# A trunk inference step: the adaLN products in 2 MB units with a weight buffer of their own

## The chip, the core and the metric

The kernel runs on one core of a Trainium2 chip. The metric is the time of one execution on the device, in microseconds: the median of three runs is 1693.69 us (1690.03 to 1694.74). One more execution was taken with the hardware profiler; all times of instructions here come from it.

## What is computed

Two groups of tokens, 128 context tokens and 256 latent tokens, go through two layers of width 1024. Each layer is a half-step SwiGLU feed-forward block, a mixer (differential attention, latent attention and a state-space path with one common input and one common output product) and a second feed-forward block. What enters each part is normed and then modulated, and what leaves it is gated, by nine vectors a layer that come from a conditioning vector:

```
def adaln(cvec, l, p):
    m = jax.nn.silu(cvec) @ p['w_ada'][l] + p['b_ada'][l]
    return m.reshape(cvec.shape[0], N_MOD, D_MODEL)

def trunk_layer(x, mod, l, p, pos, ctx):
    sh1, sc1, g1, sh2, sc2, g2, sh3, sc3, g3 = [mod[:, i, None, :] for i in range(N_MOD)]
    nw = p['norm_w'][l]
    x = x + 0.5 * g1 * swiglu(modulate(rms_norm(x, nw[0]), sh1, sc1), p['ffn_w_in'][l, 0], p['ffn_w_out'][l, 0])
    m, new_ctx = mixer(modulate(rms_norm(x, nw[1]), sh2, sc2), l, p, pos, ctx)
    x = x + g2 * m
    x = x + 0.5 * g3 * swiglu(modulate(rms_norm(x, nw[2]), sh3, sc3), p['ffn_w_in'][l, 1], p['ffn_w_out'][l, 1])
    return x, new_ctx
```

The weight `w_ada` is 1024 x 9216 in float32 for each of two layers, 72 MB in all. There are only two conditioning vectors, one for each token group, so the products have two useful columns against 75 MB of weights to be read. The shift, scale and gate of a part must exist before that part needs them, and not earlier.

## The kernel before

Activations lie transposed: 128 features on the partitions, 384 tokens along the rows, eight blocks. The large weights come as float32 and each is split into two float32r halves, `whi` by ScalarE and `wlo` by VectorE or GpSimd (`split`, L234 and L213), with two buffers for each half (`SPB`). Each product is three matmuls (`mm3`, L239 to L241). All weight loads go through `load` (L246), on the queue of SyncE (SP), into one ring of three 1 MB buffers, `raw`.

The adaLN products are made piece by piece as fillers between other work. `ada_steps` makes a list of units; each unit loads 1 MB of `w_ada` into a buffer of the ring `raw` and then multiplies. The conditioning vectors are the stationary operand, padded to 32 columns, and the weights stream. Four column groups of 32 of the array hold four stretches of columns at the same time (`ps[32*q:32*q+32]`, `q` = 0 to 3), one matmul each in turn. With 2048 output columns to a group a matmul has 512 columns and a unit four matmuls; with 1024 it has 256 and a unit eight. After the last unit of a group ScalarE copies the accumulator `adaps` (`ad`), TensorE transposes it in pieces (`adapt`) and VectorE adds the bias into `adaT`.

The very first 2048 columns are made in the opening (`start`, tile `araw`). Then 12 units are fillers of the first feed-forward block of layer 0 (eight of them together with steps that prepare tables for the state-space path), 32 of the first mixer, two of each of the next two feed-forward blocks, and 16 of the second mixer. `fill` takes the next filler off the list: the feed-forward blocks call it after each up or down step, the mixers after some input products and in each step of the attention loop.

That is the order in which the program is written. Which instruction an engine really gets next is set when the program is built: a scheduler lists the instructions of each engine and may move an independent instruction past others. Each engine works through its list in order. `tc.issue_after(x)` forbids the scheduler to place an instruction before `x`. A tile with `bufs=1` has a single buffer: who writes it next must wait until all readers of the last content are done.

The state-space path needs a table `Wi` that is written to memory and read back in another layout (`kext`, from L739; two DMAs on GpSimd's queue, tiles `kd` and `Wi`). Its first reader is the product `py` in the mixer (L1065).

Of the kernel before, what the change touches and what calls it, by code (L numbers as in the profile page):

```python
# [20 lines left out]
DEPTH = 2  # L21
# [44 lines left out]
def _layout(inp):  # L66
# [5 lines left out]
    wa = w[:, :, :8192].reshape(2, 8, 128, 4, 2048).transpose(0, 3, 1, 2, 4).reshape(2, 32, 128, 2048)  # L72
    wb = w[:, :, 8192:].reshape(2, 4, 2, 128, 1024).transpose(0, 1, 3, 2, 4).reshape(2, 4, 128, 2048)
    d['wada'] = np.concatenate([wa, wb], 1)
    for z in range(2):
        wc = w[:, :, 4096 + 1024 * z:5120 + 1024 * z].reshape(2, 4, 2, 128, 1024).transpose(0, 1, 3, 2, 4)
        d['wada'][:, 16 + 4 * z:20 + 4 * z] = wc.reshape(2, 4, 128, 2048)
    d['wada'][0, :8] = w[0, :, :2048].reshape(8, 128, 2, 8, 128).transpose(3, 1, 0, 2, 4).reshape(8, 128, 2048)
# [98 lines left out]
def trunk(ctx, tc, I, O):  # L177
# [8 lines left out]
    def bank(name):  # L186
        return psp.tile([128, 512], F32, tag="P", name=name)
# [5 lines left out]
    def SMV(n):  # L193
        return sm[:, SM[n][0]:SM[n][1]]
# [23 lines left out]
    def add(out, a, b, eng=None):  # L218
        return tt(out, a, b, ALU.add, eng)
# [13 lines left out]
    def act(out, a, f, **k):  # L233
        S.activation(out, a, f, **k)  # L234
# [8 lines left out]
    def load(src, n=2048):  # L243
        raw = wp.tile([128, 2048], F32, tag="raw", name="raw", bufs=RAWB)
        with tc.issue_after(cur.pop('dma')) if 'dma' in cur else nullcontext():
            nc.sync.dma_start(raw[:, :n], src)  # L246
        return raw

    def split(view, k, n, eng=None):
# [25 lines left out]
    adaT = [cst.tile([128, 72, 2], F32, name=f"adaT{l}") for l in range(DEPTH)]  # L275
    bada = SMV('b_ada').rearrange("p (l b) -> p l b", l=2)

    def ada_steps(l, g):
        w = 512 if g in (0, 1, 3) else 256
        units = w // 64  # L280
        row = int(8 * g)
        st = {}

        def unit(u):
            raw = load(I['wada'][l, row + u])
# [3 lines left out]
            for kk in range(8 // units):  # L289
                k = u * (8 // units) + kk  # L290
                for q in range(4):
                    c0 = kk * 1024 + q * w
                    T.matmul(ps[32 * q:32 * q + 32, 0:w], conds[:, k, :], raw[:, c0:c0 + w],  # L293
                             start=(k == 0), stop=(k == 7))
            if u == units - 1:
                ad = sp.tile([128, 512], F32, tag="ad", name="ad")
                act(ad[:, :w], ps[:, :w], AF.Copy)
                pt = bank("adapt")
                nch = w // 128
                for c in range(nch):  # L300
                    T.transpose(pt[:, c * 128:(c + 1) * 128], ad[:, c * 128:(c + 1) * 128], ident)
                b0 = 2 * row
                pv = pt[:, 0:nch * 128].rearrange("p (c q x) -> p q c x", c=nch, q=4)[:, :, :, 0:2]
                ov = adaT[l][:, b0:b0 + 4 * nch, :].rearrange("p (q c) x -> p q c x", c=nch)
                bv = bada[:, l, b0:b0 + 4 * nch].rearrange("p (q c) -> p q c", c=nch)
                for q in range(4):
                    add(ov[:, q], pv[:, q], bv[:, q, :, None].broadcast_to([128, nch, 2]))

        return [lambda u=u: unit(u) for u in range(units)]

    def mods(l, i):
        s = cst.tile([128, 8, 2], F32, name=f"mod{l}{i}")
# [333 lines left out]
    def s5_prep(l, s5p):  # L646
# [85 lines left out]
        def kext():  # L732
            o, bd = P['O'], work['bd']
            pk = bank("kext")
            pv = pk.rearrange("p (h d j) -> p h d j", h=2, d=2)
            for gp in range(8):
                for d in range(2):
                    for r in range(2):
                        T.matmul(pv[32 * (gp % 4):32 * (gp % 4) + 32, gp // 4, d, :],  # L739
                                 bd[:, r, d * 8 + gp].rearrange("p a c -> p (a c)"),  # L740
                                 o[:, r, d * 8 + gp, d:d + 8, :].rearrange("p j c -> p (j c)"),
                                 start=(r == 0), stop=(r == 1))
            kx = cur['fp'].tile([128, 2, 15, 16], F32, tag="s5raw", name="kx")
# [12 lines left out]
            nc.gpsimd.dma_start(wi.rearrange("p h g n -> p (h g) n"), win)  # L756
# [37 lines left out]
        steps += [lambda d=d, hf=hf: gtab(d, hf) for d in range(2) for hf in range(4)]  # L794
        steps += [etab]
        return P, steps

# [602 lines left out]
    def start(stp):  # L1400
# [4 lines left out]
        bv = bada[:, 0, 0:16].rearrange("p (z k) -> p z k", z=2)  # L1405
        pss = [[bank("up"), bank("up")] for _ in range(NF)]
        nx = 0
        for k in range(NB):
            while nx < min(NB, k + 1 + k // 2):
                nc.sync.dma_start(xT[:, nx], xv[:, nx])  # L1410
                norm.block(nx)
                nx += 1
            raw = stp.tile([128, 2048], F32, tag="araw", name="araw", bufs=4)
            nc.sync.dma_start(raw, I['wada'][0, k])
# [43 lines left out]
    def both(f, g):  # L1458
        return lambda: (f(), g())

    SKIP = 0
    g1 = ada_steps(0, 1)
    fillers += g1[:SKIP] + [both(f, g) for f, g in zip(g1[SKIP:], prep)] + inter(ada_steps(0, 2), prep[8 - SKIP:])

    N1, N2 = 16, 18
    
    for l in range(DEPTH):
        nx = {}

        def after_last(k):  # L1470
            if k == 0:
                nx['n'] = Norm()
            nx['n'].tail(k)
            act(xT[:, k], xT[:, k], AF.Copy, scale=SMV('fnw')[:, k:k + 1])

        def after_h(l2, i2):
            def f(k):
                if k == 0:
                    nx['n'] = Norm()
                    nx['s'], nx['sh'] = mods(l2, i2)  # L1480
                    nx['h'] = new_h()
                nx['n'].block(k)
                ffn_h_block(nx['h'], nx['s'], nx['sh'], k)
            return f

        last = l + 1 == DEPTH
        if l:
            open_ffn()
            fillers += a1[N2:]
# [7 lines left out]
        mixer(l, nx['h'], nx['n'], P, s5stack, after_h(l, 2), lazily(lambda: gates(l, 1)))  # L1497
        if not last:
            s5stack, P, prep = open_s5(l + 1)
            mid = a1[N1:N2]  # L1500
            fillers += [both(f, g) for f, g in zip(mid, prep)] + mid[len(prep):] + prep[len(mid):]
# [11 lines left out]
        (nc.sync if i % 2 else nc.scalar).dma_start(yv[:, a:b], xT[:, a:b])  # L1513


_NAMES = ('xT', 'wada', 'wfi', 'wfo', 'win', 'wout', 'wsm', 's5', 'small', 'lam', 'kc', 'vc', 'ckvc', 'kpec', 'const')


# [12 lines left out]
```

## Time and profile before

| what | us |
|---|---|
| median of three runs | 1693.69 |
| profiled execution | 1691.62 |
| its span, first to last instruction | 1689.1 |
| opening | 0 to 49.3 |
| layer 0, first feed-forward block | 49.3 to 338.7 |
| layer 0, mixer | 338.7 to 588.7 |
| layer 0, second feed-forward block | 588.7 to 882.6 |
| layer 1, first feed-forward block | 882.6 to 1165.6 |
| layer 1, mixer | 1165.6 to 1392.5 |
| layer 1, second feed-forward block, final norm | 1392.5 to 1689.1 |

The blocks are told apart by the first `up`, `pj` or `up` matmul of each. The profile shows each float32 matmul of the adaLN as two records, and a float32r matmul or a transpose as one. PE is TensorE's matmul side and PEld its weight loads, DVE is VectorE, ACT ScalarE, POOL GpSimd, SP SyncE. The ends of matmuls are modelled and overlap the next start, so that a run's time is read from the merged row.

### The profile page before, as it was taken

Reading aid. Unit: us, or ns where it says so; the run is one execution under the profiler, and the core shown is the slowest. Engines: PE = TensorE matmul, PEld = TensorE weight load, DVE = VectorE, ACT = ScalarE, POOL = GpSimd, SP = SyncE. Lnnn points to the kernel's source line nnn. Section 1 sums busy time; section 2 is a strip of 40 time slices with the busy share of each in tenths; the row PEclk is TensorE's granted clock in tenths of the full one; section 3 lists DMA queues with packets and bytes.
Section 4 is the critical chain, followed back from the end, with each engine's and each line's share of the span. In section 5 each row is a group of like instructions: output and inputs, shape, how many; then the busy total and the mean of one; then the engine's idle time right before and its main releaser. Section 6 shows DMA issues by size and latency. Waiting matters only on the chain.

```text
span 1689.1 us, 26142 instructions
## 1 busy us (share of the span) xinstructions
PE 1638.3 (97%) x10144; PEld 1491.4 (88%) x10144; DVE 1099.7 (65%) x2752; ACT 690.1 (41%) x1295; POOL 157.5 (9%) x220
## 2 busy tenths in 40 slices
PE   7999999999999999999999999999998899999997
PEld 6888999998545889999999999999974589999997
DVE  5974577758456788577575555557655766555555
ACT  4332333433455543333343333334345654333333
POOL 1220010023001400000000000001311140000000
PEclk9999999999999999999999999999999999999998
DMA  9564543443477443353344333435337133333432
GB/s 376 194 222 154 146 148 105 145 175 117 154 275 276 159 140 135 125 137 120 100 152 173 119 126 112 143 94 172 133 113 251 51 116 114 124 121 118 138 97 84
DMA packets 45931, 251.47 MB, mean 149 GB/s; under 512 B 5600, under 2 KB 10576, under 8 KB 23920
## 3 DMA queue, kind: packets, MB, share of 16 engines
q1 hardware_dynamic: 41360, 241.12, 41.4%
q0 software_dynamic: 2144, 4.54, 1.1%
q10 hardware_dynamic: 2304, 4.15, 0.8%
q8 instruction: 79, 1.29, 0.3%
q14 instruction: 44, 0.36, 0.1%
HBM read 246.73 MB, written 3.05 MB: 148 GB/s over the span
## 4 chain that ended last, share of the span: by engine, by line
PE 87%; DVE 6%; ACT 3%; DMA 2%; issue 2%; POOL 0%; ACTq 0%; SPq 0%; DVEq 0%; POOLq 0%
PE up L239 15%; PE up L241 14%; PE up L240 14%; PE down L239 7%; PE down L241 7%; PE down L240 7%; PE adaps L293 4%; PE pj L239 2%; PE pj L241 2%; PE pj L240 2%; DMA raw<-in_wada 1%; PE pout L241 1%; PE pout L239 1%; PE pout L240 1%; PE po L1174 1%
## 5 line engine op out<-in xcount | busy, mean ns | idle before, releaser
L234 ACT ACTIVATE whi<-raw 128x1024 fp32r<-128x1024 f32 (+3 forms) x360 | 332.5, 926 | 658.8 <-PE up L240 333.5
L239 PE MATMUL up<-hh,whi 128*128 128x386 f32 x1408 | 474.4, 342 | 7.8 <-ACT whi L234 4.0
L241 PE MATMUL up<-hh,wlo 128*128 128x386 f32 x1408 | 478.5, 340 | 0.6 <-DVE wlo L213 0.6
L240 PE MATMUL up<-hl,whi 128*128 128x386 f32 x1408 | 478.5, 340 | 0.0
L213 DVE TENSOR_TENSOR wlo<-raw,whi 128x1024 fp32r<-128x1024 f32 (+2 forms) x318 | 347.7, 1093 | 49.3 <-ACT whi L234 46.5
L239 PEld LDWEIGHTS up<-hh,whi 128*128 128x128 f32 x1408 | 266.2, 190 | 15.6 <-ACT whi L234 5.3
L241 PEld LDWEIGHTS up<-hh,wlo 128*128 128x128 f32 x1408 | 265.7, 189 | 9.0 <-DVE wlo L213 2.2
L240 PEld LDWEIGHTS up<-hl,whi 128*128 128x128 f32 x1408 | 266.3, 189 | 1.6 <-issue 1.1
L241 PE MATMUL down<-hidh,wlo 128*128 128x384 f32 x704 | 236.3, 336 | 0.0
L239 PE MATMUL down<-hidh,whi 128*128 128x384 f32 x704 | 235.8, 335 | 0.0
L240 PE MATMUL down<-hidl,whi 128*128 128x384 f32 x704 | 235.3, 334 | 0.0
L231 DVE SCALAR_TENSOR_TENSOR xTt<-down,gate,xTt 128x256 f32<-128x256 f32 (+1 forms) x256 | 95.1, 414 | 114.9 <-PE down L241 114.9
L466 DVE COPY bb<-up 128x2 f32<-128x2 f32 x176 | 27.8, 159 | 190.0 <-PE up L241 189.5
L241 PEld LDWEIGHTS down<-hidh,wlo 128*128 128x128 f32 x704 | 132.1, 188 | 1.1 <-issue 0.6
L239 PEld LDWEIGHTS down<-hidh,whi 128*128 128x128 f32 x704 | 132.2, 188 | 1.0 <-ACT whi L234 0.8
L240 PEld LDWEIGHTS down<-hidl,whi 128*128 128x128 f32 x704 | 132.2, 188 | 0.0
L213 DVE TENSOR_TENSOR t<-up,R 128x384 f32<-128x384 f32 x176 | 95.5, 549 | 3.3 <-ACT R L234 3.2
L293 PE MATMUL adaps<-raw,conds 128*32 128x256 f32 (+1 forms) x704 | 84.7, 498 | 3.6 <-DMA raw<-in_wada 3.6
L239 PE MATMUL pj<-hh,whi 128*128 128x386 f32 (+1 forms) x240 | 83.2, 348 | 0.9 <-ACT whi L234 0.7
L234 ACT ACTIVATE hidh<-sl 128x384 fp32r<-128x384 f32 x88 | 46.1, 524 | 91.1 <-DVE sl L231 91.1
L241 PE MATMUL pj<-hh,wlo 128*128 128x386 f32 (+1 forms) x240 | 82.1, 343 | 1.2 <-DVE wlo L213 1.2
L240 PE MATMUL pj<-hl,whi 128*128 128x386 f32 (+1 forms) x240 | 81.5, 341 | 0.0
(268 smaller groups left out, 1953.0 us busy)
## 6 DMA issues: line engine op xcount, KB each, us to landing
raw<-in_wfi SPq DMA_DIRECT2D x85, 1024.0 KB, 4.9
raw<-in_wada SPq DMA_DIRECT2D x64, 1024.0 KB, 5.7
raw<-in_wfo SPq DMA_DIRECT2D x32, 768.0 KB, 4.2
raw<-in_wfo SPq DMA_DIRECT2D x32, 640.0 KB, 3.9
raw<-in_win SPq DMA_DIRECT2D x14, 1024.0 KB, 4.8
araw<-in_wada SPq DMA_DIRECT2D x8, 1024.0 KB, 9.8
raw<-in_wout SPq DMA_DIRECT2D x16, 512.0 KB, 3.5
wr<-in_wfi SPq DMA_DIRECT2D x8, 384.0 KB, 9.7
```

The costliest lines, as they stand in the source:

```text
L213: return (eng or V).tensor_tensor(out, a, b, op=op)
L231: return V.scalar_tensor_tensor(out, a, s, b, op0=op0, op1=op1)
L234: S.activation(out, a, f, **k)
L239: T.matmul(out, whi, xhi, start=first, stop=False)
L240: T.matmul(out, whi, xlo, start=False, stop=False)
L241: marks.append(T.matmul(out, wlo, xhi, start=False, stop=last).ins)
L293: T.matmul(ps[32 * q:32 * q + 32, 0:w], conds[:, k, :], raw[:, c0:c0 + w], start=(k == 0), stop=(k == 7))
L466: V.tensor_copy(bb[:, z], ps[z][:, NT:NT + 2])
L1174: T.matmul(po[64 * h2:64 * h2 + 64, 0:256], vt[:, kt, 128 * b + 64 * h2:128 * b + 64 * h2 + 64], wTs[h2][:, kt, :], start=(kt == 0), stop= ...
```

## The change

The columns after the first 2048 of layer 0 are one list over both layers: 16384 columns in eight groups of 2048. A group is four units; a unit is a quarter of the contraction (two blocks of 128 rows), 2 MB, eight matmuls of 512 columns. The weights go into a tile `araw` with one buffer, not into the ring `raw`. The load of the next unit is a filler of its own behind each unit (`ada_load`), placed after the latest load of the ring. In the feed-forward blocks a unit's matmuls may not move ahead of the last `mm3`; in the mixers they are free (`cur['mixing']`).

```
-    def ada_steps(l, g):
-        w = 512 if g in (0, 1, 3) else 256
-        units = w // 64
+    def ada_load():
+        if pairs:
+            g, u = pairs.pop(0)
+            raw = wp.tile([128, 2, 4, 512], F32, tag="araw", name="araw", bufs=1)
+            with tc.issue_after(cur['load']):
+                nc.sync.dma_start(raw.rearrange("p k q n -> p (k q n)"), I['wada'][g, u])
+            ahead.append((g, u, raw))
...
+            with nullcontext() if cur.get('mixing') else tc.issue_after(marks[-1]):
+                for kk in range(2):
+                    for q in range(4):
+                        T.matmul(ps[32 * q:32 * q + 32], conds[:, 2 * u + kk, :], raw[:, kk, q],
+                                 start=(u == 0 and kk == 0), stop=(u == 3 and kk == 1))
+            if u == 3:
+                ad = sp.tile([128, 512], F32, tag="ad", name="ad")
+                act(ad, ps, AF.Copy)
+                pt = bank("adapt")
...
+        out = []
+        for u in range(4):
+            out += [lambda u=u: unit(u), ada_load]
+        return out
...
-            nc.gpsimd.dma_start(kd.rearrange("c h g n -> g c h n"), kx.rearrange("p h j c -> p h (j c)"))
+            nc.scalar.dma_start(kd.rearrange("c h g n -> g c h n"), kx.rearrange("p h j c -> p h (j c)"))
...
+        def kwin():
+            nc.scalar.dma_start(P['Wi'].rearrange("p h g n -> p (h g) n"), work['win'])
...
-    fillers += g1[:SKIP] + [both(f, g) for f, g in zip(g1[SKIP:], prep)] + inter(ada_steps(0, 2), prep[8 - SKIP:])
+    ada = [ada_steps(g) for g in range(8)]
+    w = ada[0] + ada[1]
+    fillers += w[:8] + [both(f, g) for f, g in zip(w[8:], prep)] + prep[8:]
...
-            fillers += ada_steps(0, 2.5) + ada_steps(0, 3) + ada_steps(0, 4)
-            a1 = ada_steps(1, 0) + ada_steps(1, 1) + ada_steps(1, 2)
-            fillers += a1[:N1]
+            fillers += ada[2] + ada[3] + ada[4] + ada[5]
         else:
-            fillers += ada_steps(1, 2.5) + ada_steps(1, 3) + ada_steps(1, 4)
+            fillers += ada[6] + ada[7]
+        cur['mixing'] = True
...
-    nc = bacc.Bacc("TRN2", target_bir_lowering=False, num_devices=1)
+    nc = bacc.Bacc("TRN2", target_bir_lowering=False, num_devices=1, dynamic_dma_scratch_size=1024)
```

So eight units (16 MB) stand in the first feed-forward block, 16 in the first mixer, eight in the second, none in the two blocks between. As the scheduler lists them, the ninth unit goes ahead into the first block and the 25th into the first mixer: nine, sixteen and seven. The two DMAs of `Wi` go to ScalarE's queue, the second one four preparation steps later, and the scratch that GpSimd's DMAs use shrinks to 1024 bytes.

The list of TensorE in the attention of the first mixer, before (`sc` scores, `wtp` transposes of the softmax, `po` the product with the values, `pk` keys; one adaLN unit is x4):

```order
L1212 MATMUL sc<-kT,qT 128x384 x4
L293 MATMUL adaps<-raw,conds 32x512 x4
L1167 MATMUL wtp<-co,e 128x128 x3
L1252 MATMUL sc<-kTh,qT_4454 128x384
L293 MATMUL adaps<-raw,conds 32x512 x4
L1167 MATMUL wtp<-co,e 128x128
L1237 MATMUL pk<-ckT,wsm 128x512
```

The same engine and part of the attention in the changed kernel, where one unit is x8 and x16 is two units with nothing between:

```order
L1224 MATMUL sc<-kT,qT 128x128 x4
L1189 MATMUL po<-wTp,vt_4436 64x128
L300 MATMUL adaps<-araw,conds 32x512 x8
L1179 MATMUL wtp<-co,e 128x128 x3
L300 MATMUL adaps<-araw,conds 32x512 x16
L307 MATMUL adapt<-co,ad 128x128 x4
L1264 MATMUL sc<-kTh,qT_4437 128x128
L1179 MATMUL wtp<-co,e 128x128 x3
```

Three units now stand within three transposes, where before units of half the size had scores and transposes between them.

Somewhat later on TensorE in the same attention, changed kernel (`npr` the norm's products, `pout` the output product):

```order
L1264 MATMUL sc<-kTh,qT_4437 128x384
L1179 MATMUL wtp<-co,e 128x128 x3
L1011 MATMUL npr<-co,tiny 64x128 x6
L300 MATMUL adaps<-araw,conds 32x512 x16
L307 MATMUL adapt<-co,ad 128x128 x4
L235 MATMUL pout<-hh_4655,whi 128x384
```

Here two units stand in a row again, and the transposes of the group follow them directly.

The queue of SP from the small weights of the mixer on, before (`raw` is the ring of three):

```order
L246 DMA raw<-in_wsm 128x1152
L246 DMA raw<-in_wada 128x2048 x16
L246 DMA raw<-in_wout 128x1024
L246 DMA raw<-in_wada 128x2048 x5
L246 DMA raw<-in_wout 128x1024
L246 DMA raw<-in_wada 128x2048 x4
L246 DMA raw<-in_wout 128x1024 x6
```

The same stretch of SP's queue in the changed kernel:

```order
L242 DMA raw<-in_wsm 128x1152
L242 DMA raw<-in_wout 128x1024 x2
L283 DMA araw<-in_wada 128x4096
L242 DMA raw<-in_wout 128x1024
L283 DMA araw<-in_wada 128x4096 x3
L242 DMA raw<-in_wout 128x1024
L283 DMA araw<-in_wada 128x4096 x7
L242 DMA raw<-in_wout 128x1024
L283 DMA araw<-in_wada 128x4096 x3
L242 DMA raw<-in_wout 128x1024 x3
```

The adaLN loads are half as many, and the output product's weights stand between them.

## Rows read from the trace of the kernel before

**Rows 1.** The page's head, busy us by engine, and GB/s in 40 slices.

```profile
span 1689.1 us, 26142 instructions
PE 1638.3 (97%) x10144; PEld 1491.4 (88%) x10144; DVE 1099.7 (65%) x2752; ACT 690.1 (41%) x1295; POOL 157.5 (9%) x220
...
GB/s 376 194 222 154 146 148 105 145 175 117 154 275 276 159 140 135 125 137 120 100 152 173 119 126 112 143 94 172 133 113 251 51 116 114 124 121 118 138 97 84
```

**Rows 2.** Busy time of each engine by stage; first column the length, last the clock.

```profile
core 0: us, PE busy (x) PEld busy (x) DVE busy (x) ACT busy (x) POOL busy (x), PEclk, DMA share, GB/s
...
338.70:588.70 250.00, 241.01 (x1610) 172.04 (x1609) 158.54 (x464) 112.22 (x278) 52.84 (x52) 0.98 0.54 191
...
882.60:1165.60 283.00, 283.00 (x1632) 280.61 (x1631) 168.64 (x335) 109.10 (x168) 4.13 (x17) 1.00 0.39 132
1165.60:1392.50 226.90, 212.24 (x1474) 167.12 (x1473) 149.11 (x439) 110.11 (x277) 51.40 (x51) 0.98 0.39 134
```

**Rows 3.** The same by stage for instructions on the tile adaps alone.

```profile
49.30:338.70 289.40, 18.76 (x128) 3.82 (x128) 0.00 (x0) 0.98 (x2) 1.00 0.48 158
338.70:588.70 250.00, 43.34 (x320) 8.48 (x320) 0.00 (x0) 2.56 (x5) 0.98 0.54 191
588.70:882.60 293.90, 2.14 (x32) 0.83 (x32) 0.00 (x0) 0.00 (x0) 1.00 0.41 132
882.60:1165.60 283.00, 2.75 (x32) 0.94 (x32) 0.00 (x0) 0.39 (x1) 1.00 0.39 132
1165.60:1392.50 226.90, 17.70 (x192) 4.71 (x192) 0.00 (x0) 1.39 (x3) 0.98 0.39 134
```

**Rows 4.** Timeline of PE: start, time of a run, the run (two records a matmul).

```profile
49.36 1.06 PE L293 MATMUL adaps<-raw,conds 128*32 128x512 f32 x8
...
493.61 1.92 PE L293 MATMUL adaps<-raw,conds 128*32 128x512 f32 x16
...
496.70 1.05 PE L293 MATMUL adaps<-raw,conds 128*32 128x512 f32 x4
```

**Rows 5.** DMA issues: tile, queue, count, size, median us from issue to landing.

```profile
raw<-in_wfi SPq DMA_DIRECT2D x85, 1024.0 KB, 4.9
raw<-in_wada SPq DMA_DIRECT2D x64, 1024.0 KB, 5.7
raw<-in_wfo SPq DMA_DIRECT2D x32, 768.0 KB, 4.2
...
Wi<-kd POOLq DMA_DIRECT2D x2, 1024.0 KB, 22.5
```

**Rows 6.** Timeline of PE: three transposes of the softmax in the first mixer.

```profile
537.90 0.49 PE L1167 MATMUL wtp<-co,e 128*128 128x128 f32 x3
```

**Rows 7.** Busy time by stretch within the first mixer, columns as in Rows 2.

```profile
412.00:416.00 4.00, 2.58 (x23) 1.58 (x22) 3.88 (x9) 2.85 (x8) 0.00 (x0) 0.98 0.10 25
416.00:420.00 4.00, 4.00 (x24) 3.15 (x22) 0.18 (x1) 1.87 (x4) 0.59 (x1) 0.60 0.97 328
450.00:500.00 50.00, 46.28 (x300) 22.04 (x298) 26.45 (x99) 28.80 (x80) 1.54 (x3) 0.97 0.73 264
500.00:560.00 60.00, 58.69 (x374) 32.06 (x373) 39.40 (x139) 30.93 (x93) 10.01 (x10) 1.00 0.69 247
```

**Rows 8.** Timeline of PE: an adaLN run that waits, with idle time and releaser.

```profile
515.41 0.82 PE L1167 MATMUL wtp<-co,e 128*128 128x128 f32 x6
517.27 1.07 PE L293 MATMUL adaps<-raw,conds 128*32 128x512 f32 x8 [1.05 <-DMA raw<-in_wada]
```

**Rows 9.** Timeline of PE: transposes directly behind a group's last matmul.

```profile
198.73 1.06 PE L293 MATMUL adaps<-raw,conds 128*32 128x256 f32 x14
200.29 0.44 PE L301 MATMUL adapt<-co,ad 128*128 128x128 f32 x2 [0.49 <-ACT ad L234]
```

**Rows 10.** Reader and loader of Wi: count, min/median/max ns, first and last start.

```profile
L1065 PE MATMUL py<-Wi,U x64: 272/310/449, 415.3 to 1252.0; 128*48 128x128 f32 x64
```

More of the change, by code (lines that the diff above doesn't have):

```diff
@@ L71, in _layout @@
     w = a['w_ada']
[L72 to L78, printed above, removed]
+    d['wada0'] = w[0, :, :2048].reshape(8, 128, 2, 8, 128).transpose(3, 1, 0, 2, 4).reshape(8, 128, 2048)
+    w = np.concatenate([w[0, :, 2048:], w[1]], 1)
+    d['wada'] = w.reshape(4, 2, 128, 8, 2048).transpose(3, 0, 2, 1, 4).reshape(8, 4, 128, 4096)
     d['wfi'] = a['ffn_w_in'].reshape(2, 2, 8, 128, 2, NJ, 128).transpose(0, 1, 5, 3, 2, 4, 6).reshape(2, 2, NJ, 128, 2048)
@@ L245, in load @@
         with tc.issue_after(cur.pop('dma')) if 'dma' in cur else nullcontext():
-            nc.sync.dma_start(raw[:, :n], src)
+            cur['load'] = nc.sync.dma_start(raw[:, :n], src).ins
         return raw
@@ L274, in trunk, with ada_steps @@
     act(conds[:, :, 0:2], SMV('cond').rearrange("p (k c) -> p k c", c=2), AF.Silu)
-    adaT = [cst.tile([128, 72, 2], F32, name=f"adaT{l}") for l in range(DEPTH)]
-    bada = SMV('b_ada').rearrange("p (l b) -> p l b", l=2)
-    def ada_steps(l, g):
-        w = 512 if g in (0, 1, 3) else 256
-        units = w // 64
-        row = int(8 * g)
+    adaA = cst.tile([128, 144, 2], F32, name="adaA")
+    adaT = [adaA[:, 72 * l:72 * l + 72] for l in range(DEPTH)]
+    bada = SMV('b_ada')
+    pairs = [(g, u) for g in range(8) for u in range(4)]
+    ahead = []
+    def ada_load():
[5 more added lines that the diff above has]
+            ahead.append((g, u, raw))
+    def ada_steps(g):
         st = {}
         def unit(u):
-            raw = load(I['wada'][l, row + u])
+            if not ahead:
+                ada_load()
+            g_, u_, raw = ahead.pop(0)
+            assert (g, u) == (g_, u_)
             if u == 0:
@@ L288, in unit @@
             ps = st['ps']
-            for kk in range(8 // units):
-                k = u * (8 // units) + kk
-                for q in range(4):
[L292 to L309, printed above, removed]
+            with nullcontext() if cur.get('mixing') else tc.issue_after(marks[-1]):
[7 more added lines that the diff above has]
+                pt = bank("adapt")
+                for c in range(4):
+                    T.transpose(pt[:, c * 128:(c + 1) * 128], ad[:, c * 128:(c + 1) * 128], ident)
+                b0 = 16 + 16 * g
+                pv = pt.rearrange("p (c q x) -> p q c x", c=4, q=4)[:, :, :, 0:2]
+                ov = adaA[:, b0:b0 + 16, :].rearrange("p (q c) x -> p q c x", c=4)
+                bv = bada[:, b0:b0 + 16].rearrange("p (q c) -> p q c", c=4)
+                for q in range(4):
+                    add(ov[:, q], pv[:, q], bv[:, q, :, None].broadcast_to([128, 4, 2]))
+        out = []
+        for u in range(4):
+            out += [lambda u=u: unit(u), ada_load]
+        return out
     def mods(l, i):
@@ L755, in kext @@
             win = bass.AP(tensor=src.tensor, offset=src.offset, ap=[[16, 8], list(src.ap[0]), list(src.ap[1]), [1, 128]])
-            nc.gpsimd.dma_start(wi.rearrange("p h g n -> p (h g) n"), win)
+            work['win'] = win
             P['Wi'] = wi
+        def kwin():
+            nc.scalar.dma_start(P['Wi'].rearrange("p h g n -> p (h g) n"), work['win'])
         def etab():
@@ L793, in s5_prep @@
         steps += [kext]
-        steps += [lambda d=d, hf=hf: gtab(d, hf) for d in range(2) for hf in range(4)]
+        steps += [lambda d=d, hf=hf: (gtab(d, hf), kwin() if (d, hf) == (0, 3) else None) for d in range(2) for hf in range(4)]
         steps += [etab]
@@ L1404, in start @@
         av = adaT[0][:, 0:16, :].rearrange("p (z k) x -> p z k x", z=2)
-        bv = bada[:, 0, 0:16].rearrange("p (z k) -> p z k", z=2)
+        bv = bada[:, 0:16].rearrange("p (z k) -> p z k", z=2)
         pss = [[bank("up"), bank("up")] for _ in range(NF)]
@@ L1412, in start @@
                 nx += 1
-            raw = stp.tile([128, 2048], F32, tag="araw", name="araw", bufs=4)
-            nc.sync.dma_start(raw, I['wada'][0, k])
+            raw = stp.tile([128, 2048], F32, tag="araw0", name="araw0", bufs=4)
+            nc.sync.dma_start(raw, I['wada0'][k])
             wr = stp.tile([128, NF, 256], F32, tag="wr", name="wr", bufs=4)
@@ L1459, in both @@
         return lambda: (f(), g())
-    SKIP = 0
-    g1 = ada_steps(0, 1)
-    fillers += g1[:SKIP] + [both(f, g) for f, g in zip(g1[SKIP:], prep)] + inter(ada_steps(0, 2), prep[8 - SKIP:])
-    N1, N2 = 16, 18
+    ada = [ada_steps(g) for g in range(8)]
+    w = ada[0] + ada[1]
+    fillers += w[:8] + [both(f, g) for f, g in zip(w[8:], prep)] + prep[8:]
     for l in range(DEPTH):
@@ L1488, in trunk @@
             open_ffn()
-            fillers += a1[N2:]
         ffn(l, 0, h, norm, lazily(lambda: gates(l, 0)), after_h(l, 1), 0, () if l else pss)
         if l == 0:
-            fillers += ada_steps(0, 2.5) + ada_steps(0, 3) + ada_steps(0, 4)
-            a1 = ada_steps(1, 0) + ada_steps(1, 1) + ada_steps(1, 2)
-            fillers += a1[:N1]
-        else:
-            fillers += ada_steps(1, 2.5) + ada_steps(1, 3) + ada_steps(1, 4)
+            fillers += ada[2] + ada[3] + ada[4] + ada[5]
+        else:
+            fillers += ada[6] + ada[7]
+        cur['mixing'] = True
         mixer(l, nx['h'], nx['n'], P, s5stack, after_h(l, 2), lazily(lambda: gates(l, 1)))
+        cur['mixing'] = False
         if not last:
             s5stack, P, prep = open_s5(l + 1)
-            mid = a1[N1:N2]
-            fillers += [both(f, g) for f, g in zip(mid, prep)] + mid[len(prep):] + prep[len(mid):]
+            fillers += prep
         open_ffn()
@@ L1513, in trunk @@
         (nc.sync if i % 2 else nc.scalar).dma_start(yv[:, a:b], xT[:, a:b])
-_NAMES = ('xT', 'wada', 'wfi', 'wfo', 'win', 'wout', 'wsm', 's5', 'small', 'lam', 'kc', 'vc', 'ckvc', 'kpec', 'const')
+_NAMES = ('xT', 'wada0', 'wada', 'wfi', 'wfo', 'win', 'wout', 'wsm', 's5', 'small', 'lam', 'kc', 'vc', 'ckvc', 'kpec', 'const')
 def kernel(**inputs):
```

## The prediction

> **What bounds the kernel now.** I read the totals first: TensorE is busy 97% of a span of 1689.1 us, the next engine (VectorE) 65% [rows 1]. So a change counts if it shortens or stops TensorE. Next the table by stage [rows 2]: the feed-forward block of the second layer is busy for all its 283.00 us, the first mixer for 241.01 of 250.00, the second for 212.24 of 226.90. Even in the mixers little is free: 9.0 and 14.7 us. The same stretches for the adaLN accumulator alone [rows 3] say what the work to be moved costs: 18.76, 43.34, 2.14, 2.75 and 17.70 us. The timeline tells how it costs [rows 4]: the profile shows two records for each of these matmuls, which go to four column groups in turn; a run of four matmuls of 512 columns (eight records) takes 1.06 us, of two matmuls 1.05, of eight 1.92. Short runs pay for groups that stand empty. Last the loads [rows 5]: 1 MB lands 4.9 us after its issue, 0.75 MB after 4.2; an adaLN load, often beside others, after 5.7.
>
> **Matmul runs.** Columns and bytes stay; 704 records become 512, and a unit becomes eight matmuls. Where the new order leaves a unit whole it costs 1.92 us, in pieces the sum of its runs. By that order: first feed-forward block, nine units, eight whole and one as 5+1+2: 8 x 1.92 + 1.92 + 2 x 1.05 = 19.4, against 18.76: +0.6. First mixer, sixteen units: twelve whole (23.0), then 3+3+2 (3.15), 1+7 (2.97), 1+1+1+5 (5.07), 5+1+2 (4.02): 38.2 against 43.34: -5.1. The two blocks between the mixers lose theirs: -2.1 and -2.8. Second mixer, seven units, five whole (9.6), 2.97 and 5.07: 17.6 against 17.70: -0.1. Sum -9.5; bounds -23 (all 32 units whole: 61.4 against 84.7) and -4.9 (the blocks between alone). TensorE is nearly full there, so I count it all.
>
> **The wait that is added.** The old loads share a ring of three 1 MB buffers. The new buffer is one: a unit's 2 MB load can be issued only when the last matmul of the unit before has read it, and TensorE takes instructions in order. So two units closer together than a load takes make TensorE stand. The order of the first mixer has this at three places: a unit, three transposes, a unit, a unit directly behind it; later once more two in a row. What is queued behind them is the attention itself (scores, transposes, the output product), and with it the next block. A 2 MB load is not in the trace. Bounds: 2.1 MB at the busiest rate of any slice, 376 GB/s [rows 1], takes 5.6 us without any fixed part; twice 5.7 is 11.4. From 0.75 to 1 MB the landing grows by 0.7 us [rows 5], 2.8 per MB, so I take 4.9 + 2.8 = 7.7. The three transposes hide 0.49 [rows 6]: 7.2 + 7.7 + 7.7 = 22.6 us. Could TensorE have been idle there anyway? From 500 to 560 us it is busy 58.69 of 60.00 [rows 7], so hardly 1 us. And the ring of three already ends one wait with an adaLN load, 1.05 us at 517.27 [rows 8], while DMA is busy 0.69 to 0.73 of the time [rows 7]. The Trainium skill, page "DMA: Bandwidth & Descriptors", section "Anatomy of one DMA — SWDGE (gpsimd) path", gives about 2.0 us plus bytes at 436 GB/s, as an estimate 6.8 us a load, 20 us for the three and 1710 for the kernel. For 1 MB it would give 4.4 where rows 5 have 4.9 on the hardware queue, so I leave it.
>
> The other neighbours in the attention stand further apart; between none (0) and one whole load (8) of exposure in sum, I take +3. In the feed-forward blocks two units have 96 matmuls between them, at 283.00 / 1632 = 0.173 us [rows 2] 16.6 us, more than a load: 0. If that cover went, each of eight units could cost the 7.7.
>
> **Transposes behind the last unit.** At four places the four transposes of a group now follow its last matmul directly and wait for ScalarE's copy. In the old order that happens once visibly: 0.49 us of idle time [rows 9]. Four such, with the wider copy, 2 to 4; one is paid already: +2.
>
> **The clock.** In the first mixer the granted clock is 0.98, a loss of 5 us over 250 [rows 2]. From 412 to 416 us TensorE is busy 2.58 of 4.00, and from 416 to 420 the clock is 0.60 with the engine busy throughout [rows 7]: 3.2 us at the lower of 1.2 and 2.4 GHz, 1.6 us lost. Three waits longer than that idle time should bring three such stretches, 4.8, partly inside the wait itself, and some of the old ones may move: 0 to +10, I take +3. The Trainium skill speaks against the change here: "TensorE: Matmul & The Clock Gate", section "HAM oscillation — how this bites in real kernels", tells of bursts of matmuls that each start at the low clock because a DMA wait stands before them. By that rule the term is the full 4.8 and the kernel 1715. Rows 7 agree that idle time goes before the fall; no run shown here has a wait as long.
>
> **The rest.** While TensorE stands, the other engines catch up: -1 (0 to -3, since only some 1 us of later idle time is there to win). The table DMA Wi takes 22.5 us to land [rows 5] and moves from GpSimd's queue to ScalarE's, later in the block, but its first reader starts only at 415.3 [rows 10], some 77 us into the mixer: 0. ScalarE waits for the first of the two DMAs with splits queued behind it that TensorE needs; two split buffers hide that: 0 to +5, taken 0. The smaller scratch for GpSimd's DMAs is not visible in the trace; GpSimd is busy 52.84 of 250.00 [rows 2]: 0 to +3, taken 0. The ring of three that now belongs to the other weights alone can gain nothing where TensorE is never idle: 0 to -2, taken 0.
>
> **Sum.** -9.5 + 22.6 + 3 + 2 + 3 - 1 = +20.1 us. The profiled execution took 1691.6 (its span of 1689.1 and 2.5 around it); that gives 1711.7. The median of the three runs, 1693.7, lies 2.1 higher, so the same sum on it gives 1713.8; I say 1713.
>
> **Rivals.**
> (a) The load chain sets the pace of the whole attention, not three places of it. Loads of 11.4 us (beside weight loads on the same queue, which also stand behind waiting adaLN loads): 3 x 11.4 = 34, the other neighbours 12, clock 5: -9.5 + 34 + 12 + 2 + 5 = +43, 1735. It decides once a 2 MB load takes over some 10 us. For it: DMA busy 0.69 to 0.73 in this stretch. Against: few other loads are left there, and 1 MB alone lands in 4.9.
> (b) Faster. The waits fall where the attention's own chain is late, so that the two units in a row cost nothing: -9.5, and 2 from the clock, 1680 to 1682. It decides once less than 9.5 of the 22.6 us is exposed. For it: 9.0 us idle in the first mixer, and units stand in pairs where a scheduler saw nothing else to issue. Against it: 58.69 of 60.00 busy in just that stretch.
> (c) Both cancel: the saving gets half way to its bound (-16), the loads cost their lower bound of 5.6 each (17), the small terms 2: +3, 1694 to 1697. It needs pieces that pack as well as whole units, against rows 4.
>
> **How the numbers follow.** Forecast 0.62, its own range 1703 to 1724 (waits 16 to 29 and the small terms); (a) 0.18; (b) 0.10; (c) 0.10. Some 0.3% (5 us) is what a measurement of this kernel can tell from no change. Slower by more: forecast, (a) and a little of (c), 0.82. Same: most of (c), 0.08. Faster: (b), 0.10. The range runs from 1694, inside (c), to 1734, nearly the whole of (a); left out are (b) and a tail above.
>
> **What would show it.** The waits of TensorE should list adaLN matmuls waiting for the araw load, three of them 7 to 9 us long between some 510 and 600 us, and little else new; the first mixer 265 to 280 us long, the second within 3 us of 226.90, the two blocks between them some 2 us shorter each. The adaLN records should be 512, busy some 75 us outside the opening (before 84.7). The 2 MB load should land in about 7.7. Granted clock in the first mixer 0.97 or less. I am wrong if no wait exceeds 4 us, if the first mixer is not longer than 250, or if the blocks between grow.

## The result and the profile after

The changed kernel takes 1731.3 us (median; runs from 1729.7 to 1741.3) against 1692.2 for the kernel before on the same chip: ratio 1.0243, 95% interval 1.0200 to 1.0285, slower by 39 us. The forecast was 1713 with a range of 1694 to 1734: the sign and the place are right, the size is half. The result lies inside the stated range and above the forecast's own range, 1703 to 1724.

The profiled execution of the first series took 1741.3 us, ten more than the median. I ran the kernel once more for a profile near the median (e5: 1731.5 us, span 1729.7), and make the sum with that one. Both show the same waits.

The totals of e5, which answer to [rows 1]:

```profile
span 1729.7 us, 25680 instructions
PE 1637.5 (95%) x9952; PEld 1488.2 (86%) x9952; DVE 1096.8 (63%) x2740; ACT 688.6 (40%) x1292; POOL 153.2 (9%) x216
```

TensorE is busy 0.8 us less than before in a span 40.6 us longer: the loss looks like nothing but idle time, until the clock is read below. By stage, e5, columns as in [rows 2] (first feed-forward block, first mixer, the two blocks between, second mixer, last block):

```profile
49.30:342.30 293.00, 289.03 (x1719) 268.74 (x1720) 202.51 (x486) 108.34 (x173) 33.37 (x51) 1.00 0.51 173
342.30:632.00 289.70, 244.93 (x1545) 172.71 (x1545) 156.18 (x457) 111.65 (x278) 53.43 (x52) 0.93 0.45 164
632.00:923.50 291.50, 289.17 (x1694) 286.54 (x1693) 216.51 (x528) 116.74 (x187) 4.69 (x22) 1.00 0.41 126
923.50:1204.00 280.50, 280.07 (x1598) 279.61 (x1598) 168.33 (x330) 108.71 (x167) 4.15 (x17) 1.00 0.38 125
1204.00:1432.90 228.90, 213.07 (x1392) 165.13 (x1391) 147.45 (x435) 109.78 (x275) 51.17 (x51) 0.99 0.34 123
```

First mixer 289.7 against 250.0: +39.7, and the clock fell from 0.98 to 0.93. The first block is 3.6 us longer, the blocks between 2.4 and 2.5 shorter, the second mixer 2.0 longer. The adaLN accumulator alone, for [rows 3], in the first block and the two mixers:

```profile
49.30:342.30 293.00, 19.39 (x144) 1.00 0.51 173
342.30:632.00 289.70, 47.06 (x256) 0.93 0.45 164
1204.00:1432.90 228.90, 18.99 (x112) 0.99 0.34 123
```

The first block has the 19.4 of the forecast to the tenth. The first mixer has 47.06 where 38.2 were forecast. The group of the adaLN matmuls and its load, from the page of e5 (busy, mean ns, then the idle time before them; last the median landing):

```profile
L300 PE MATMUL adaps<-araw,conds 128*32 128x512 f32 x512 | 85.4, 683 | 27.5 <-DMA araw<-in_wada 27.5
...
araw<-in_wada SPq DMA_DIRECT2D x32, 2048.0 KB, 7.5
```

And where the longest of those waits lie: the timeline of TensorE in the first profile of the changed kernel (start, length, the run; in brackets the idle time and what ended it):

```profile
527.47 1.92 PE L300 MATMUL adaps<-araw,conds 128*32 128x512 f32 x16
529.33 0.55 PE L1179 MATMUL wtp<-co,e 128*128 128x128 f32 x3
537.10 3.61 PE L300 MATMUL adaps<-araw,conds 128*32 128x512 f32 x16 [7.22 <-DMA araw<-in_wada]
548.23 3.64 PE L300 MATMUL adaps<-araw,conds 128*32 128x512 f32 x16 [7.53 <-DMA araw<-in_wada]
...
583.06 3.64 PE L300 MATMUL adaps<-araw,conds 128*32 128x512 f32 x16 [1.10 <-DMA araw<-in_wada]
594.54 3.64 PE L300 MATMUL adaps<-araw,conds 128*32 128x512 f32 x16 [7.84 <-DMA araw<-in_wada]
```

Three waits of 7.22, 7.53 and 7.84 us, 22.6 in sum: just the places and the sum that the forecast gave (22.2 in e5). Read the second column too: the unit that didn't wait takes 1.92 us, those behind a wait 3.6, the same run at half speed (1.2 of 2.4 GHz). So the loss of the clock stands in the busy time of the engine, not in its idle time, and the totals hide it.

All waits for a load in the first mixer, e5 and then the kernel before (sum, times, longest):

```profile
PE adaps L300 <- DMA araw<-in_wada: 26.5, 7, 7.7
PE adaps L293 <- DMA raw<-in_wada: 2.1, 3, 1.0
```

### The profile page after: what moved, and what is told of

The parts are those of the page before. It is cut to its first block, busy times and chain, and to the rows that moved or that the text cites. A ratio compares the mean times of both kernels' runs of the same rounds, so it can differ in the third digit from the quotient of the medians.

```text
span 1739.5 us, 25680 instructions
## 1 busy us (share of the span) xinstructions
PE 1648.2 (95%) x9952; PEld 1495.0 (86%) x9952; DVE 1096.8 (63%) x2740; ACT 688.7 (40%) x1292; POOL 151.6 (9%) x216
## 4 chain that ended last, share of the span: by engine, by line
PE 84%; DVE 7%; DMA 3%; ACT 3%; issue 2%; POOL 0%; SPq 0%; DVEq 0%; ACTq 0%; POOLq 0%
PE up L235 13%; PE up L236 13%; PE up L237 13%; PE down L235 7%; PE down L237 7%; PE down L236 7%; PE adaps L300 5%; DMA araw<-in_wada 3%; PE pj L235 2%; PE pj L237 2%; PE pj L236 2%; PE pout L237 1%; PE sc L1224 1%; PE pout L235 1%; PE pout L236 1%
## 5 line engine op out<-in xcount | busy, mean ns | idle before, releaser
L300 PE MATMUL adaps<-araw,conds 128*32 128x512 f32 x512 | 87.9, 702 | 26.9 <-DMA araw<-in_wada 26.9
```

The source lines that it names most:

```text
L300: T.matmul(ps[32 * q:32 * q + 32], conds[:, 2 * u + kk, :], raw[:, kk, q], start=(u == 0 and kk == 0), stop=(u == 3 and kk == 1))
```

## The experiments

My theory, T1: a single buffer makes TensorE stand a whole load wherever a unit follows a unit. Rivals: the loads as a whole pace the mixers (R2), the free placement (R3), the small parts of the change (R4), the adaLN matmuls lowering the clock by themselves (R1).

**e1: the same memory as two buffers of 1 MB.**

```diff
-raw = wp.tile([128, 2, 4, 512], F32, tag="araw", name="araw", bufs=1)
+raw = [wp.tile([128, 4, 512], F32, tag="araw", name="araw", bufs=2) for _ in range(2)]
...
-nc.sync.dma_start(raw.rearrange("p k q n -> p (k q n)"), I['wada'][g, u])
+for kk in range(2):
+    nc.sync.dma_start(raw[kk].rearrange("p q n -> p (q n)"), I['wada'][g, u, :, 2048 * kk:2048 * kk + 2048])
...
-T.matmul(ps[32 * q:32 * q + 32], conds[:, 2 * u + kk, :], raw[:, kk, q],
+T.matmul(ps[32 * q:32 * q + 32], conds[:, 2 * u + kk, :], raw[kk][:, q],
```

> The changed kernel, with the unit's 2 MB brought by two 1 MB loads into two buffers of 1 MB each (the same memory): the first half can be refilled when the first four of a unit's eight matmuls have run. T1 (one buffer of 2 MB makes TensorE stand a whole load time of 7.7 us wherever a unit follows a unit, and the low clock comes behind those waits): adaLN waits fall from 26.9 us to under 8, the half-speed stretches of the first mixer from some 55 us to under 20, time 1692 to 1705. R1 (adaLN matmuls themselves, in runs of eight, make the clock fall): waits go, clock stays at 0.91 to 0.95 in the first mixer, time 1705 to 1715. R2 (the total of 64 MB in the mixers is too much for the loads): waits stay at 20 us or more, time 1725 to 1735.

Measured: 1689.2 us, ratio to before 0.9989 (0.9978 to 1.0000). The group of the adaLN matmuls on the page of e1:

```profile
L301 PE MATMUL adaps<-araw,conds 128*32 128x512 f32 x512 | 79.8, 611 | 5.5 <-DMA araw<-in_wada 5.3
```

The first mixer of e1, columns as in [rows 2]:

```profile
343.60:593.50 249.90, 240.66 (x1544) 169.34 (x1544) 156.94 (x457) 112.03 (x277) 53.29 (x52) 0.99 0.54 191
```

Load waits 5.3 instead of 27.5, the first mixer at 249.9, its clock at 0.99. The whole loss of the change goes when the one 2 MB buffer becomes two of 1 MB, though all 64 MB still come over the same queue: R2 falls. R1 isn't decided here, since the scheduler broke the units up: of 37 adaLN runs in this mixer all but three have four matmuls or fewer. e6 decides it. The number of buffers and the size of a piece change together; no run gave whole units a second 2 MB buffer. The time is below T1's range by 3 us; so the new layout has at most a small advantage over the old, 2.6 us with an interval that reaches none, not the 9.5 that the forecast wrote down for the runs.

**e2: units in the mixers held behind the last `mm3` written before them.**

```diff
-        cur['mixing'] = True
+        cur['mixing'] = False
```

> The changed kernel, with the units inside the mixers held to their place in the program as in the feed-forward blocks (not free to be placed by the scheduler). T1 (the single buffer): the units still stand close together, waits of 15 to 30 us stay, time 1722 to 1738. R3 (the free placement is what puts unit behind unit): waits under 8 us, time 1693 to 1708.

Measured: 1738.9 us, ratio 1.0284 (1.0266 to 1.0302); load waits 28.3 us, the first mixer 289.5 at a clock of 0.92. T1's waits are met, its time is passed by 1 us. R3 isn't decided by it: from 443 to 549 us TensorE runs no `mm3` in e2, so the hold had nothing to hold to in most of the attention, and two units still stand in a row at 532 and at 578 us. That the places of the units matter is seen in e9.

**e3: two of the four column groups moved out of the first mixer.**

```diff
         if l:
             open_ffn()
+            fillers += ada[5]
...
-            fillers += ada[2] + ada[3] + ada[4] + ada[5]
+            fillers += ada[2] + ada[3]
...
-            fillers += prep
+            fillers += ada[4] + prep
```

> The changed kernel with one buffer, but with only two column groups (eight units) in the first mixer, one in the feed-forward block after it and one in the block after that. T1: fewer units in the attention of the first mixer, so waits of 0 to 10 us in it and none in the blocks (a unit has 16 us of matmuls behind it there): first mixer 255 to 265 us, the two blocks 292 to 296 and 283 to 286, time 1698 to 1712. R2 (loads as a whole): the waits follow the units into the blocks, time 1720 to 1735.

Measured: 1706.2 us, ratio 1.0102 (1.0059 to 1.0146). The load waits are 2.3 us in the whole program, as T1 said. The time is in T1's range too, but that is luck, for the stages I had wrong, and the errors cancel:

```profile
342.60:573.00 230.40, 213.36 (x1392) 165.57 (x1391) 151.93 (x446) 110.35 (x275) 52.97 (x52) 0.99 0.37 134
573.00:874.00 301.00, 298.00 (x1763) 288.56 (x1762) 216.73 (x534) 117.77 (x188) 5.00 (x22) 1.00 0.45 150
874.00:1168.30 294.30, 293.15 (x1682) 281.98 (x1681) 168.87 (x335) 109.60 (x168) 4.14 (x17) 1.00 0.43 148
1168.30:1406.80 238.50, 222.36 (x1392) 170.36 (x1391) 147.73 (x435) 110.87 (x275) 51.19 (x51) 0.94 0.33 118
```

The mixer shrinks to 230, the blocks grow to 301 and 294. And in the mixer 17.0 us of idle time are left (230.40 - 213.36) though hardly any of it is a load: with 112 records of adaLN in place of 256, its small waits show (the kernel before has 9.0 in all). That was the first sign of a second cost. The second mixer, at a clock of 0.94, is 10 us longer than in e5.

**e4: the small parts alone**, on the kernel before.

```diff
-nc.gpsimd.dma_start(kd.rearrange("c h g n -> g c h n"), kx.rearrange("p h j c -> p h (j c)"))
+nc.scalar.dma_start(kd.rearrange("c h g n -> g c h n"), kx.rearrange("p h j c -> p h (j c)"))
...
-nc.gpsimd.dma_start(wi.rearrange("p h g n -> p (h g) n"), win)
+work['win'] = win
...
+def kwin():
+    nc.scalar.dma_start(P['Wi'].rearrange("p h g n -> p (h g) n"), work['win'])
...
-nc = bacc.Bacc("TRN2", target_bir_lowering=False, num_devices=1)
+nc = bacc.Bacc("TRN2", target_bir_lowering=False, num_devices=1, dynamic_dma_scratch_size=1024)
```

> The kernel before, with only the small parts of the change: the two table DMAs on ScalarE's queue instead of GpSimd's, the second of them later, and the smaller scratch for GpSimd's DMAs. T1: within 2 us of the kernel before (1690 to 1695). R4 (these parts bring the loss in the second mixer, where few loads wait): 1698 to 1706, the second mixer 5 us longer or more.

Measured: 1692.0 us against 1691.8, ratio 1.0006 (0.9993 to 1.0020). Two of the three terms that the forecast took as 0, the queue of `Wi` and the scratch, are 0. The third, the ring that the other weights have to themselves, is not in this run: here the adaLN loads still go through it.

**e5: the changed kernel again**, unedited.

> The changed kernel once more, for a second profile: the first profiled execution took 1741 us, 10 more than the median of its runs. T1: the same three load waits of 7 to 8 us in the first mixer, the same runs of adaLN matmuls, and fewer half-speed stretches of TensorE's clock than the 55 us of the first profile; time 1728 to 1736. If the loss were in the clock alone, the waits would shrink with the time; they should not.

Measured: 1731.5 us, load waits 27.5, the three long ones 6.8, 7.7 and 7.6. Between the two profiles the waits stay and the clock moves. The second mixer in the first profile:

```profile
1206.50:1442.80 236.30, 220.71 (x1393) 169.64 (x1393) 147.52 (x435) 109.99 (x276) 51.17 (x51) 0.95 0.34 120
```

against 228.90 with a clock of 0.99 in e5: the idle time is the same (15.6 and 15.8), the busy time 7.6 longer. At 0.95 some 236.3 x 0.05 x 2 = 24 us run at half speed, at 0.99 some 5: up to (24 - 5) / 2 = 9.5 us of lost work, an estimate that covers it.

**e6: work in the waits.** Fourteen added matmuls behind each unit whose successor waits.

```diff
+    warm = cst.tile([128, 4, 32], F32, name="warm")
...
-                        T.matmul(ps[32 * q:32 * q + 32], conds[:, 2 * u + kk, :], raw[:, kk, q],
+                        m = T.matmul(ps[32 * q:32 * q + 32], conds[:, 2 * u + kk, :], raw[:, kk, q],
...
+            if 4 * g + u in (17, 18, 22):
+                with tc.issue_after(m.ins), tc.high_priority():
+                    for i in range(14):
+                        T.matmul(ps[:, 0:256], warm.rearrange("p q c -> p (q c)"), co[:, 0:256], start=False, stop=False)
```

> The changed kernel with fourteen further matmuls of 128x256 directly behind each of the three units whose successor waits for its load (units 17, 18 and 22; they read constants and add into rows of the accumulator that nobody reads). They are some 6 us of TensorE work in each wait of 7 to 8 us: the load waits shrink to 1 to 2 us, the units start when they did. C1 (TensorE's idle time in the waits makes the clock fall behind them): the stretches at half speed from 530 us to the end of the first mixer, 38 us before, go to under 10, first mixer 278 to 286 us, kernel 1716 to 1726, faster than the changed kernel although it does 18 us more work. C2 (the adaLN matmuls themselves, or the work around them, make it fall): half-speed stretches stay, the added matmuls run at half speed too, kernel 1731 to 1750.

Measured: 1730.3 us (1727.0 to 1731.7), ratio to before 1.0232 (1.0215 to 1.0249). The timeline of TensorE in e6 at the place of the first two waits, and the unit behind the third:

```profile
527.65 1.92 PE L303 MATMUL adaps<-araw,conds 128*32 128x512 f32 x16
529.50 6.31 PE L308 MATMUL adaps<-co,warm 128*128 128x256 f32 x28
538.23 1.92 PE L303 MATMUL adaps<-araw,conds 128*32 128x512 f32 x16 [2.09 <-DMA araw<-in_wada]
540.09 6.31 PE L308 MATMUL adaps<-co,warm 128*128 128x256 f32 x28
547.64 1.92 PE L303 MATMUL adaps<-araw,conds 128*32 128x512 f32 x16 [1.25 <-DMA araw<-in_wada]
...
589.74 1.92 PE L303 MATMUL adaps<-araw,conds 128*32 128x512 f32 x16 [1.24 <-DMA araw<-in_wada]
```

The stretch of the first two waits in e5 and in e6; the clock is the number before the last two:

```profile
530.00:560.00 30.00, 13.78 (x75) 6.02 (x79) 5.09 (x24) 5.63 (x17) 1.88 (x2) 0.77 0.55 211
530.00:560.00 30.00, 25.95 (x151) 18.97 (x154) 6.98 (x28) 6.84 (x20) 3.04 (x4) 1.00 0.56 211
```

The first mixer of e6, and in it the added matmuls alone:

```profile
342.40:627.80 285.40, 260.40 (x1629) 188.13 (x1628) 154.50 (x457) 111.00 (x277) 53.21 (x52) 0.96 0.45 167
342.40:627.80 285.40, 18.93 (x84) 15.71 (x84) 0.96 0.45 167
```

C1 has the cause: with TensorE busy in the wait, the three units behind it, at 538, 547 and 589 us, take 1.92 us again instead of 3.3 to 3.6, and the clock between 530 and 560 is 1.00 instead of 0.77. R1 falls too: these are runs of eight matmuls at full speed. The first mixer is inside C1's range, 285.4 us instead of 289.7, and its busy time without the added matmuls is 3.5 us shorter (260.40 - 18.93 = 241.47, against 244.93). The kernel's time is not in C1's range but 4 us above it: the median is some 1 us below e5, and the spread of the runs is larger than that. One unit still runs at half speed there: the one at 578 us takes 3.62 behind a wait of 1.96.

The Trainium skill's page "TensorE: Matmul & The Clock Gate", section "HAM oscillation — how this bites in real kernels", tells of matmuls that start at the low clock because a DMA wait stands before them. For these three places the trace agrees with the rule: 3.3 to 3.6 us behind the waits, 1.92 where the wait is filled.

**e7 and e8: the matmuls of a unit tied together.** In e1 the scheduler still breaks a half of four matmuls into pieces. e7 is e1 and e8 the kernel before, each with all matmuls of one load queued behind its first.

```diff
+with tc.issue_after(first) if q else nullcontext(), tc.high_priority() if q else nullcontext():
-    T.matmul(ps[32 * q:32 * q + 32], conds[:, 2 * u + kk, :], raw[kk][:, q],
+    m = T.matmul(ps[32 * q:32 * q + 32], conds[:, 2 * u + kk, :], raw[kk][:, q],
...
+if q == 0:
+    first = m.ins
```

> As the kernel with two loads of 1 MB into two buffers (e1), with the four matmuls of a half queued directly behind each other, so that the scheduler can't put other work between them. T5 (a run of one to three matmuls costs 1.05 us like a run of four, so split halves are paid twice): adaLN busy outside the opening from 79.8 to 66 to 70 us, kernel 1676 to 1684. R5 (the pieces fill gaps in which TensorE would be idle anyway): busy time falls, idle time rises by as much, kernel 1687 to 1692.

> The kernel before, with the matmuls of each 1 MB unit queued directly behind each other, and nothing of the change. T5: adaLN busy from 83 to 66 to 72 us, kernel 1675 to 1684: then what the change was to win in matmul runs is had without it. R5: 1689 to 1694.

Measured: e7 1675.7 us, ratio 0.9909 (0.9894 to 0.9924); e8 1675.5, ratio 0.9910 (0.9895 to 0.9925). The adaLN accumulator in the first mixer of e7, columns as in [rows 3]:

```profile
341.10:579.30 238.20, 34.70 (x256) 0.99 0.56 200
```

The same of e8:

```profile
331.10:570.00 238.90, 33.61 (x320) 0.99 0.55 199
```

Against 43.34 of [rows 3], with as many columns: 9 us in this stage, and the mixer is 11 to 12 shorter. Outside the opening the sum is 66.9 and 68.1 instead of 84.7. T5 holds for both; e7's time is 0.3 us below its range. The two beat both kernels by 16 and 56 us, and they are equal: what the change could win in runs is had without it, by an order.

**e9: one buffer, tied.** The changed kernel with all eight matmuls of a unit behind its first.

```diff
+with tc.issue_after(first) if q + kk else nullcontext(), tc.high_priority() if q + kk else nullcontext():
-    T.matmul(ps[32 * q:32 * q + 32], conds[:, 2 * u + kk, :], raw[:, kk, q],
+    m = T.matmul(ps[32 * q:32 * q + 32], conds[:, 2 * u + kk, :], raw[:, kk, q],
...
+if q + kk == 0:
+    first = m.ins
```

> The changed kernel with its one buffer of 2 MB, with the eight matmuls of a unit queued directly behind each other. By the order of its instructions only one unit of the first mixer still stands directly behind another. T1 (each such pair costs TensorE one load of 7.5 us, and the rest of the loss follows the places of the units): load waits 9 to 13 us instead of 26.5, first mixer 256 to 268 us, kernel 1698 to 1712; between the two tied kernels and the changed one. R2 (the single buffer paces all units): waits over 20 us, kernel over 1718.

Measured: 1701.1 us, ratio 1.0064 (1.0041 to 1.0088). First mixer 261.2, and the two largest of TensorE's waits there (sum, times, longest):

```profile
PE adaps L301 <- DMA araw<-in_wada: 9.5, 2, 7.5
PE rot L868 <- ACT pjt L230: 2.4, 1, 2.4
...
```

One pair, one wait of 7.5 (and 2.0 once): T1 as written. The matmuls are busy as little as in e7 (34.8 in this mixer), but the kernel is 25 us slower than e7, with 9.5 in load waits. The rest is small waits of the attention itself (the mixer's idle time is 28.6; without the loads 19.1, in e7 9.0 in all) and the clock (0.94, in e7 0.99). With the same single buffer the changed kernel loses 39 us and this one 10: the buffer costs where a unit stands behind a unit, and it is the order that the scheduler chose which put them there. So a part of R3 holds.

**e10: the table steps of the first block as early as before.**

```diff
-    fillers += w[:8] + [both(f, g) for f, g in zip(w[8:], prep)] + prep[8:]
+    fillers += [both(f, g) for f, g in zip(w[:8], prep)] + inter(w[8:], prep[8:])
```

> The changed kernel with the table steps of the first feed-forward block handed out as in the kernel before (one with each of the first eight steps, then in turn). T6 (the later table steps make the small waits of that block, 4.0 us of idle time against 0.5 before): block 289 to 291 us instead of 292.9, idle under 2.5. R6 (the ninth unit and the transposes behind units make it longer): block 292 to 294, idle 3.5 to 4.5. Kernel 1726 to 1736 by either.

Measured: 1733.6 us, the block 295.0 us with 4.2 idle, at a clock of 0.99. T6 falls: the waits stay when the table steps move. R6 has the idle time and misses the block by 1 us. The ninth unit isn't the reason, for e2's first block holds only eight and is idle 4.15 us. The transposes behind units are a part: in e5 1.4 us of waits, 0.5 before. Two of the others, 0.63 and 0.58 us, lie at 50.5 and 55.7 us in the first profile of the changed kernel, whose first unit in this block starts at 64.40; the kernel before has units at 49.36 and 55.68.

## Why the forecast was right in kind and half in size

Terms of the sum against e5 (span 1729.7 against 1689.1: +40.6):

| term | forecast | measured |
|---|---|---|
| waits for loads, first mixer (26.5 against 2.1) | 22.6 + 3 | +24.4 |
| transposes behind the last unit (measured: first mixer) | +2 | +1.8 |
| other idle time in the first mixer (16.5 against 6.9) | -1 | +9.6 |
| TensorE's busy time there (244.93 against 241.01): runs, clock | -5.1 + 3 | +3.9 |
| first feed-forward block | +0.6 | +3.6 |
| the two blocks between | -4.9 | -4.9 |
| second mixer | -0.1 | +2.0 |
| last block | 0 | +0.3 |
| queue of Wi, scratch | 0 | 0 (e4) |
| ring of three | 0 | not measured alone |

Right: the added wait, its three places, its length, and its cause. The load time of 7.7 us, worked out from two sizes, was measured as 7.4 to 7.8 (medians of the runs with one buffer). The Trainium skill's page "DMA: Bandwidth & Descriptors", section "Anatomy of one DMA — SWDGE (gpsimd) path", would give 6.8, an estimate for another queue; it was rightly left. Right too are the runs in the first block, the work that the blocks between lose, and the two zeros that e4 tests. Rival (a) named nearly the time, 1735, but not the reason: loads took 7.5, not 11.4, and nothing but the pairs waits long for them. That the stated range, which ends at 1734, holds the result is owed to this rival: the range was drawn to take it in. Of the signs, the first mixer (265 to 280, measured 289.7) and the adaLN busy time outside the opening (75, measured 85.4) were missed.

Wrong was the step "While TensorE stands, the other engines catch up: -1 ... only some 1 us of later idle time is there to win". It saw idle time that could be won, not idle time that the adaLN runs were covering. In the kernel before, a run stands in front of the transposes that wait for ScalarE:

```profile
473.58 1.07 PE L293 MATMUL adaps<-raw,conds 128*32 128x256 f32 x16
474.96 0.53 PE L1291 MATMUL qt2p<-co,qt 128*96 128x128 f32 x3 [0.30 <-ACT qt L234]
476.02 1.07 PE L293 MATMUL adaps<-raw,conds 128*32 128x256 f32 x16 [0.53 <-DMA raw<-in_wada]
477.02 0.53 PE L1291 MATMUL qt2p<-co,qt 128*96 128x128 f32 x3
```

In e5 only one unit of 2 MB stands there, between the two groups of these transposes, and both wait in the open:

```profile
470.51 0.83 PE L1303 MATMUL qt2p<-co,qt 128*96 128x128 f32 x6 [1.71 <-DVE qt L209]
...
474.32 1.92 PE L300 MATMUL adaps<-araw,conds 128*32 128x512 f32 x16 [1.04 <-DMA araw<-in_wada]
...
481.83 0.86 PE L1303 MATMUL qt2p<-co,qt 128*96 128x128 f32 x6 [1.30 <-ACT qt L230]
```

Such small waits make the +9.6. Three runs speak for it: e3, with seven units in this mixer and hardly any load wait, has them; e9, with whole units, has 19.1 us of them; e1 and e7, with pieces of 1 MB from two buffers each, lose them (9.2 and 9.0 us of idle time in all). The first block's +3.5 of idle time is 0.9 for transposes behind units, which belongs to the forecast's +2; the rest is of the same kind by its places, which is not shown, for no run put a unit back at its start.

The clock was mis-sized: I took 3. The adaLN runs of the first mixer came out in just the pieces that were counted, 38.2 us at full speed, and took 47.06: 8.9 more. All other work of the stage takes what it did (244.93 - 47.06 = 197.87, against 197.67). The runs of e5 that are slowest for their length:

```profile
448.14 3.63 PE L300 MATMUL adaps<-araw,conds 128*32 128x512 f32 x14
463.87 2.79 PE L300 MATMUL adaps<-araw,conds 128*32 128x512 f32 x16
...
536.78 3.64 PE L300 MATMUL adaps<-araw,conds 128*32 128x512 f32 x16 [6.83 <-DMA araw<-in_wada]
548.15 3.31 PE L300 MATMUL adaps<-araw,conds 128*32 128x512 f32 x16 [7.73 <-DMA araw<-in_wada]
...
581.27 3.26 PE L300 MATMUL adaps<-araw,conds 128*32 128x512 f32 x16 [1.14 <-DMA araw<-in_wada]
592.16 3.49 PE L300 MATMUL adaps<-araw,conds 128*32 128x512 f32 x16 [7.63 <-DMA araw<-in_wada]
```

Against 1.92 each, the three behind the long waits lost 1.72, 1.39 and 1.57 us, 4.7 in sum, next to the 4.8 that the forecast worked out and did not write. The other 4.2 are the unit at 581 us (1.3), the runs at 448 and 463 us (2.6) and small change. Why the clock was low there is open: no run was made for it, the kernel before has one slow run near the same place (3.04 us at 444.23), and e1, without most of the small waits, has a clock of 0.99 over the stage.

Of the saving of 9.5 in runs the 4.9 of the blocks between showed; the 5.1 of the first mixer the clock took back. In e1, where no long wait spoils it but the units are broken up further, adaLN is busy 79.8 against 84.7 and the kernel gains 2.6 at most. The real lever in the runs was that a load's matmuls were broken apart. [rows 4] said so (1.05 us for two matmuls, 1.06 for four), and I used it for a term and not for a question.

## What to carry to other kernels

Filler work does two jobs: it costs its own time, and it covers the waits of the chain it is placed in. Before making fillers larger or their buffer single, list the small waits that stand directly behind them, and ask what stands there when the next filler isn't loaded yet; half-size pieces in two buffers of the same memory kept both jobs here (1689 against 1731). And where short runs pay for groups that stand empty, tie the matmuls of one load together: 16 us here, without any new layout.

## What the hardware showed that I had not expected

- The clock fell also where TensorE, by the profile, was busy all the time. In the first profile of the changed kernel it goes from 1.00 to 0.50 at 445.0 us, behind 6.80 us with 6.80 busy (first two rows). In the long wait it is back at 0.99 while the engine has next to nothing to do (fourth row), and falls again behind it (fifth):

```profile
438.20:445.00 6.80, 6.80 (x37) 4.86 (x35) 4.08 (x13) 4.59 (x13) 2.55 (x2) 1.00 0.06 27
445.00:451.80 6.80, 6.80 (x29) 2.72 (x29) 4.40 (x19) 2.17 (x7) 0.51 (x1) 0.50 0.24 79
533.70:540.50 6.80, 3.40 (x16) 0.59 (x16) 0.00 (x0) 0.00 (x0) 0.00 (x0) 0.50 0.34 147
540.50:543.90 3.40, 0.20 (x4) 0.00 (x0) 0.00 (x0) 0.00 (x0) 0.00 (x0) 0.99 0.64 202
543.90:557.60 13.70, 8.65 (x35) 5.61 (x36) 1.64 (x9) 1.42 (x4) 0.61 (x1) 0.50 0.60 232
```

- Two executions of one kernel differ by ten us (1731.5 and 1741.3) with the same waits; 7.4 of it is the second mixer, by its clock of 0.99 and 0.95.
- 18.9 us of added TensorE work (e6) cost nothing that could be measured, because it stood in waits (medians 1730.3 and 1731.3).
